# A hybrid attention and DeltaNet layer: one more pair of projections, one pass fewer, and two steps moved

## The chip, the cores and the metric

The kernel runs on one core of one Trainium2 chip. The metric is the time on the device in microseconds (us); TensorE does the matmuls, VectorE (DVE), ScalarE (ACT) and GpSimd (POOL) the elementwise work, SyncE (SP) issues most DMAs. Each engine has a queue of its own, filled in the order in which the program was written; semaphores hold an instruction until its inputs are there.

## What is computed

The reference, cut to what matters for this change:

```python
h = rms_norm(x, norm_g)                      # x: 768 tokens (512 + 256) of 2048 numbers
proj = einsum('bsd,dp->bsp', h, w_in)        # 8192 + 32 columns
aq, ak, av, ag, dq, dk, dv, dg, b_raw, a_raw = split(proj)
# attention: 8 heads x 128 from aq, ak, av, times silu(ag)
# DeltaNet:  8 heads x 128 from dq, dk, dv, times silu(dg); decay and beta per head and token:
beta = sigmoid(b_raw)
g = -exp(a_log) * softplus(a_raw + dt_bias)  # summed over a chunk, then exp: the decays
y = rms_norm(x + concat(attn, dn) @ w_out, final_gain)
```

All matmuls of the projection split both factors in two float32r parts (hi and lo) and add three products: hi by hi, hi by lo, lo by hi.

## The kernel before

x is kept transposed: 16 tiles of 128 rows (model dimension) by 768 tokens, each as `xh[k]` and `xl[k]`. `x_split` makes them from the landing buffer `xstage[k]` and multiplies by the norm gain `g_in` on the way (ScalarE for the high part, VectorE for the low one). The landing buffer itself keeps the plain x, for the sums of squares. The root of the mean square is applied to the results, by `rB`, a row of 768 factors that `start_rms` makes behind the first pass.

The 64 weight tiles of 128 columns are projected in four ways, in this order:

1. `project_two` with `ab=True`: two DeltaNet gates (tiles 56, 57) and the 32 columns for beta and decays (`ab_step`), tile of x by tile of x as they land. `arrivals` splits and squares each tile.
2. `project_two` again: gates 58, 59 (pass 2, `after="raw"`).
3. `project_two` again: q and k of attention head 0 (pass 3, `after="std"`).
4. `pair_products`: ten pairs of weight tiles, each in two halves (`ph`) of eight x tiles. A half uses seven products in place of eight, a Strassen-Winograd scheme over two blocks of tokens and two blocks of the model dimension. Its products (`PRODUCTS`) go into three PSUM banks X, Y, Z. `evacuate` takes each product out before the next one of the same bank starts. The products 4 to 7 multiply sums of x blocks, T1 to T4.
5. `project`: the convolution inputs of the DeltaNet and the other q and k, one tile at a time, beside which the attention and the scan run.

`block_sums(ph, i)` makes T1 to T4 for the x tiles a = 8 ph + i and a + 4, eight blocks in all. For one block it stores the second half of `xh[a]`, `xl[a]` to DRAM (`bD`), multiplies the two landing buffers by `g_in` (ScalarE), and then does four differences, four casts to the high part (ScalarE) and four low parts (VectorE). T2 takes the place of the second half of `xh[a]` and `xl[a]`, so it waits until the pass that counts in `reached["std"]` has used tile a:

```python
if n == "T2":
    yield from wait(lambda: reached["std"] > a)
    d[n] = xh[a][:, hi], xl[a][:, hi]
```

The others go to free landing buffers, listed in `PLACES`. At the last pair, `restore` loads the stored halves back.

The order of the instructions is planned while the program is built. `Driver` keeps a clock for each engine with the costs of `Engine.cost`. Side work is a set of generators, spawned with a priority (lower goes first): `follow` and `evacuate` -20, `arrivals` -10, `all_sums` -8, `spill_post`'s store -7, `gating` (beta and decays) -4. At each slot between matmuls, up to three steps of those that are due are written out. `yield AHEAD` lets a step go on 2 us before its own end by that plan, `yield 0` only at its end. Engines then run their queues in the order written.

`gating` waits for `rB`, multiplies the `ab` columns by it, transposes them on TensorE (`pg`), and does some 30 small operations on `scr` (96 columns) on VectorE with a few on ScalarE in between. Its last steps are small matmuls for the chunk sums and three exponentials. What it makes is used from the scan on, behind the pairs.

Of the kernel before, what the change touches and what calls it, by code (L numbers as in the profile page):

```python
# [16 lines left out]
T = 768  # L17
TP, TS = 512, 256
NT = T // P
NH = 8  # L20
# [32 lines left out]
AHEAD = 2.0  # L53
DEEP = 2.5
PAIRED = 0
# [202 lines left out]
def encoder_kernel(tc, x, xT, wt, wab, wo, convw, gain, dngain, fgain, alog, dtb, cst, tabs, y):  # L258
# [43 lines left out]
    with (  # L302
# [62 lines left out]
        if True:  # L365
# [67 lines left out]
            def arrivals():  # L433

                for k in range(NK):
# [3 lines left out]
                    for c in parts if k == 0 else (slice(0, T),):  # L439
                        x_split(k, c)  # L440
# [145 lines left out]
            reached = {"raw": 0, "std": 0, "left": 0}  # L586
# [159 lines left out]
            def block_sums(ph, i):  # L746
# [8 lines left out]
                for k in (a, a + 4):  # L755
                    A.mul(xstage[k], xstage[k], g_in[:, k:k + 1])
                yield AHEAD
# [17 lines left out]
                def low(n, E=V):  # L775
# [20 lines left out]
            PLACES = (("t16", "t17", "t18"), ("t19", "t20", "t21"), ("t22", "t23", "t0"), ("t4", "t1", "t5"), ("t2", "t6", "t3"),  # L796
                      ("t7", "t8", "t12"), ("t9", "t13", "t10"), ("t14", "t11", "t15"))
# [99 lines left out]
            def gating():  # L897
                ident, ones = C["ident"], C["ones"]
                yield from wait(lambda: "rms" in flags)
                yield from get("t23", "f768", "sa")  # L900
                scr = st("t23", (7, 2 * nd), "scr")
                ab = f768("ab")
                w1, w2, w3, w4, gg = (scr[:, j].rearrange("p (d t h) -> p d t h", d=2, t=NT) for j in (0, 1, 2, 3, 6))
                raw = scr[:, 4:6].rearrange("p b (d t h) -> p b d t h", d=2, t=NT)
# [60 lines left out]
                give("t23", "sa")  # L965
# [532 lines left out]

            pairs += [(h, NH + h) for h in range(NH - PAIRED, NH)]
            kinds += [(("q", h), ("k", h)) for h in range(NH - PAIRED, NH)]  # L1500
            attn = [(f, spill_post(kind, h)) for h in range(NH - PAIRED) for f, kind in ((h, "q"), (NH + h, "k"))]
            first, attn = attn[:2], attn[2:]
# [13 lines left out]
            plan_raw([f for f, _ in first])  # L1516
# [47 lines left out]
            drv.end = 0.0  # L1564
            spawn(arrivals(), -10)
            spawn(start_rms(), -30)
            project_two((raw_gate_post(0, "t19"), raw_gate_post(1, "t20")), raw_hook, ab=True)
            give("t16", "t17", "t18")
            spawn(all_sums(), -8)
            spawn(gating(), -4)  # L1570
            project_two((raw_gate_post(2, "t21"), raw_gate_post(3, "t22")), lambda k: None, "raw")
            project_two([p for _, p in first], lambda k: None, "std")

            def pair_hook(pi):
                def hook(ph, pr):
# [243 lines left out]
```

## Time and profile before

| | us |
|---|---|
| median of 3 runs | 1657.13 |
| lowest, highest | 1653.51, 1657.84 |
| the profiled execution | 1661.15 |
| its span (first to last instruction) | 1659.4 |
| mean granted TensorE clock in it | 0.985 of full speed |

The profile shows one execution on one core. "Busy" is the time in which an engine executes; an instruction's row gives its start from the span's start, its length, and in brackets the idle time ahead of it on its engine with what ended it. The ends of matmuls are modelled and overlap the next one's start, so their listed length is longer than the distance from one to the next.

### The profile page before, as it was taken

To read this page: it belongs to the slowest core of one execution; us is meant where nothing else is said; L and a number is where in the kernel's file an instruction comes from. 1 tells how busy PE (TensorE), PEld (TensorE's weight loads), DVE (VectorE), ACT (ScalarE), POOL (GpSimd) and SP (SyncE) were. 2 spreads that over 40 slices of the span, in tenths; PEclk is the share of its full clock that TensorE was granted. 3 is DMA by queue.
4 is the path that set the end of the run, shared out by engine and by line. 5 is a ranking of instruction groups with operands and counts; after the bars stand their busy time and mean duration, and the time that the engine had idled before them with its cause. 6 is when DMAs were issued, how large, how long until landed. Compare 5 with 4: busy or idle time off the path is not lost.

```text
span 1659.4 us, 30160 instructions
## 1 busy us (share of the span) xinstructions
PE 1597.8 (96%) x11675; PEld 1411.5 (85%) x11675; DVE 934.0 (56%) x2003; ACT 799.6 (48%) x1800; POOL 237.2 (14%) x233
## 2 busy tenths in 40 slices
PE   7998999999999999999999999999999889999995
PEld 6887999999888898988888888888878678887874
DVE  6558877778445554556555555665355555444332
ACT  6655333434354565556455656545355554433322
POOL 0000000000222221222213121312110011111220
PEclk9998999999999999999999999999999899999998
DMA  6232232323423323222223332232335455646557
GB/s 244 80 122 86 99 105 94 110 89 116 164 83 91 83 71 94 79 78 92 78 67 92 100 80 75 77 84 91 102 125 178 149 172 172 194 137 225 156 171 276
DMA packets 135265, 198.51 MB, mean 120 GB/s; under 512 B 49393, under 2 KB 60241, under 8 KB 135121
## 3 DMA queue, kind: packets, MB, share of 16 engines
q1 hardware_dynamic: 133968, 193.43, 36.2%
q10 hardware_dynamic: 1152, 3.15, 0.5%
q8 instruction: 92, 1.51, 0.4%
q14 instruction: 53, 0.43, 0.1%
HBM read 150.08 MB, written 46.45 MB: 118 GB/s over the span
## 4 chain that ended last, share of the span: by engine, by line
PE 80%; DMA 6%; DVE 5%; issue 4%; ACT 3%; POOL 1%; SPq 1%; ACTq 0%; DVEq 0%; POOLq 0%
PE mm L286 36%; PE mmo L286 8%; PE mmY L286 7%; PE mmr L286 7%; PE c L286 5%; PE mmX L286 5%; PE mmZ L286 5%; PE m L286 2%; DMA out_y<-row 2%; DMA st<-in_wo 1%; PE kk L286 1%; PE o L286 1%; DMA ak<-kD 1%; PE S L286 1%; DMA res<-in_x 1%
## 5 line engine op out<-in xcount | busy, mean ns | idle before, releaser
L286 PE MATMUL mm<-xl_x,hip 128*128 128x512 f32 (+1 forms) x1152 | 307.2, 348 | 0.0
L286 PE MATMUL mm<-xh_x,lop 128*128 128x512 f32 (+1 forms) x1152 | 305.5, 346 | 0.0
L286 PE MATMUL mm<-xh_x,hip 128*128 128x512 f32 (+1 forms) x1152 | 304.5, 345 | 0.0
L204 ACT CAST hip<-st 128x512 fp32r<-128x512 f32 x244 | 150.9, 619 | 236.8 <-PE mm L286 74.2
L204 POOL TENSOR_TENSOR lop<-st,hip 128x512 fp32r<-128x512 f32 x72 | 97.3, 1351 | 928.4 <-ACT hip L204 826.3
L204 DVE TENSOR_TENSOR lop<-st,hip 128x512 fp32r<-128x512 f32 x172 | 120.9, 703 | 193.8 <-ACT hip L204 188.6
L286 PEld LDWEIGHTS mm<-xh_x,hip 128*128 128x128 f32 x1152 | 176.5, 189 | 22.8
L286 PEld LDWEIGHTS mm<-xh_x,lop 128*128 128x128 f32 x1152 | 176.6, 189 | 21.7
L286 PEld LDWEIGHTS mm<-xl_x,hip 128*128 128x128 f32 x1152 | 176.4, 189 | 21.2
L286 PE MATMUL mmr<-xh_x,raw 128*128 128x512 f32 (+1 forms) x512 | 118.5, 345 | 11.3 <-ACT xh_x L204 9.6
L204 DVE SCALAR_TENSOR_TENSOR cacc<-cin,cw,cacc 128x772 f32<-128x772 f32 x96 | 107.4, 1119 | 23.4 <-ACT cacc L204 22.0
L204 ACT ACTIVATE s<-s,m 128x512 f32<-128x512 f32 (+1 forms) x96 | 61.5, 648 | 97.5 <-DVE m L204 97.4
L286 PEld LDWEIGHTS mmr<-xh_x,raw 128*128 128x128 f32 x512 | 79.7, 191 | 25.3 <-ACT xh_x L204 9.9
L286 PE MATMUL mmo<-oh,xh_m 128*128 128x512 f32 x192 | 79.2, 412 | 4.6 <-DVE q L204 4.1
L286 PE MATMUL mmo<-oh,mh 128*128 128x512 f32 x192 | 76.6, 399 | 1.8 <-ACT mh L204 1.6
L286 PE MATMUL mmo<-ol,xh_m 128*128 128x512 f32 x192 | 76.8, 400 | 1.0 <-POOL ol L204 0.5
L286 PE MATMUL mmo<-ol,mh 128*128 128x512 f32 x192 | 76.6, 399 | 0.6 <-DVE ol L204 0.5
L286 PE MATMUL mmo<-oh,ml 128*128 128x512 f32 x192 | 76.6, 399 | 0.3 <-DVE ml L204 0.3
L286 PE MATMUL mmo<-oh,xl_m 128*128 128x512 f32 x192 | 76.2, 397 | 0.0
L286 PE MATMUL mmr<-xl_x,raw 128*128 128x512 f32 (+1 forms) x256 | 67.0, 343 | 0.4 <-DVE xl_x L204 0.4
L204 ACT ACTIVATE z<-c,rho 128x128 f32<-128x128 f32 x96 | 35.1, 367 | 66.6 <-PE c L286 66.5
L204 DVE TENSOR_TENSOR res<-mmo,res 128x512 f32<-128x512 f32 x42 | 28.8, 687 | 67.5 <-PE mmo L286 46.3
(256 smaller groups left out, 3287.0 us busy)
## 6 DMA issues: line engine op xcount, KB each, us to landing
st<-in_wt SPq DMA_DIRECT2D x256, 256.0 KB
st<-in_wo SPq DMA_DIRECT2D x64, 256.0 KB
dec<-gcD SPq DMA_DIRECT2D x24, 256.0 KB
res<-in_x SPq DMA_DIRECT2D x24, 256.0 KB
yD<-res SPq DMA_DIRECT2D x24, 256.0 KB
res<-yD SPq DMA_DIRECT2D x24, 256.0 KB
out_y<-row SPq DMA_DIRECT2D x12, 512.0 KB
xst<-in_xT SPq DMA_DIRECT2D x15, 384.0 KB
```

Source lines behind the costliest of these rows:

```text
L204: r = f(*a, **k)
L286: r = PE.matmul(out, lhsT, rhs, start=start, stop=stop, skip_group_check=more)
```

## The change

- `PAIRED = 1`: q and k of head 0 become an eleventh pair, at the end of the pairs, in place of the third pass. `reached["std"]` is counted by the second pass now.
- `scales()`, a generator of its own at priority -7, multiplies the landing buffers by `g_in` as soon as their squares are taken. `block_sums` waits for two entries of `scaled` in place of doing it.
- `gating` waits for the flag `tset` (all block sums written out) in place of `rms`, and its scratch is in two `half` buffers in place of `t23`.
- The first part of x tile 0 is split ahead of the tasks; gates 2 and 3 go to `f768` buffers in place of `t21`, `t22`; `PLACES` is a new list.

```diff
-PAIRED = 0
+PAIRED = 1
@@ arrivals
-                    for c in parts if k == 0 else (slice(0, T),):
-                        x_split(k, c)
+                    x_split(k, slice(0, T) if k else parts[1])
@@ block_sums
-                for k in (a, a + 4):
-                    A.mul(xstage[k], xstage[k], g_in[:, k:k + 1])
-                yield AHEAD
+                yield from wait(lambda: {a, a + 4} <= scaled)
@@ new
+            scaled = set()
+
+            def scales():
+
+                for k in (0, 4, 1, 5, 2, 6, 3, 7, 8, 12, 9, 13, 10, 14, 11, 15):
+                    yield from wait(lambda: sq[0] > k)
+                    A.mul(xstage[k], xstage[k], g_in[:, k:k + 1])
+                    scaled.add(k)
+                    yield AHEAD
+
-            PLACES = (("t16", "t17", "t18"), ("t19", "t20", "t21"), ("t22", "t23", "t0"), ...
+            PLACES = (("t16", "t17", "t18"), ("t21", "t22", "t0"), ("t4", "t1", "t5"), ...
@@ gating
-                yield from wait(lambda: "rms" in flags)
-                yield from get("t23", "f768", "sa")
-                scr = st("t23", (7, 2 * nd), "scr")
+                yield from wait(lambda: "tset" in flags)
+                yield from get("half", "half", "f768", "sa")
+                scr, scr2 = (st("half", (4, 2 * nd), n) for n in ("scr", "scr2"))
@@ the lists of pairs and of single tiles
-            pairs += [(h, NH + h) for h in range(NH - PAIRED, NH)]
-            kinds += [(("q", h), ("k", h)) for h in range(NH - PAIRED, NH)]
-            attn = [(f, spill_post(kind, h)) for h in range(NH - PAIRED) for f, kind in ((h, "q"), (NH + h, "k"))]
-            first, attn = attn[:2], attn[2:]
+            pairs += [(h, NH + h) for h in range(PAIRED)]
+            kinds += [(("q", h), ("k", h)) for h in range(PAIRED)]
+            attn = [(f, spill_post(kind, h)) for h in range(PAIRED, NH) for f, kind in ((h, "q"), (NH + h, "k"))]
@@ the passes
+            x_split(0, parts[0])
             spawn(arrivals(), -10)
             spawn(start_rms(), -30)
+            spawn(scales(), -7)
             project_two((raw_gate_post(0, "t19"), raw_gate_post(1, "t20")), raw_hook, ab=True)
             give("t16", "t17", "t18")
             spawn(all_sums(), -8)
             spawn(gating(), -4)
-            project_two((raw_gate_post(2, "t21"), raw_gate_post(3, "t22")), lambda k: None, "raw")
-            project_two([p for _, p in first], lambda k: None, "std")
+            project_two((raw_gate_post(2, "f768"), raw_gate_post(3, "f768")), lambda k: None, "std")
```

## Rows read from the trace of the kernel before

**Rows 1.** The page, part 1: busy time, share of the span, instructions.

```profile
PE 1597.8 (96%) x11675; PEld 1411.5 (85%) x11675; DVE 934.0 (56%) x2003; ACT 799.6 (48%) x1800; POOL 237.2 (14%) x233
```

**Rows 2.** Windows by stage: from:to, length, busy time of each engine with its instructions, granted TensorE clock, share of the DMA engines, GB/s. Nearly all of pass 2; pass 3; pair 0 in two halves; pair 1.

```profile
63.49:97.20 33.71, 33.38 (x198) 29.12 (x198) 13.80 (x42) 13.35 (x34) 0.00 (x0) 1.00 0.25 80
96.30:130.19 33.89, 33.89 (x193) 29.23 (x192) 23.15 (x50) 22.09 (x43) 0.00 (x0) 1.00 0.38 125
130.19:155.11 24.92, 19.25 (x86) 18.51 (x85) 21.38 (x41) 13.32 (x25) 0.00 (x0) 0.80 0.33 113
155.11:171.88 16.77, 15.62 (x86) 14.76 (x85) 15.36 (x30) 8.07 (x15) 0.00 (x0) 0.99 0.22 76
171.88:200.98 29.10, 29.10 (x168) 28.86 (x168) 22.51 (x39) 9.84 (x17) 0.00 (x0) 1.00 0.29 101
```

**Rows 3.** Waits of TensorE from 0 to 200 us: who waited for whom, total us, times, longest.

```profile
PE mmr L286 <- ACT xh_x L204: 9.6, 1, 9.6
PE mmX L286 <- ACT sum L204: 3.5, 1, 3.5
PE mmY L286 <- DVE out L204: 2.7, 2, 2.2
...
PE mmY L286 <- DVE xl_x L204: 0.5, 1, 0.5
PE mmr L286 <- DVE xl_x L204: 0.4, 1, 0.4
```

**Rows 4.** TensorE's instructions in order of time, around pair 0: start, length, what, and in brackets the idle time ahead with its releaser.

```profile
132.11 0.34 PE L286 MATMUL mmX<-xh_x,lop 128*128 128x384 f32 x1
135.96 0.69 PE L286 MATMUL mmX<-xh_x,hip 128*128 128x384 f32 x1 [3.51 <-ACT sum L204]
...
137.09 0.52 PE L286 MATMUL mmX<-xh_x,hip 128*128 128x384 f32 x1
...
169.69 0.59 PE L286 MATMUL mmY<-T4s,hip 128*128 128x384 f32 x2 [0.58 <-DVE out L204]
```

**Rows 5.** VectorE's instructions in order of time, first and last ones of some blocks of the sums (T1f to T4f are the differences, T1s to T4s the low parts).

```profile
62.91 0.55 DVE L204 TENSOR_TENSOR T1f<-xst 128x384 f32<-128x384 f32 x1
...
103.36 0.55 DVE L204 TENSOR_TENSOR T4s<-T4f,T4s 128x384 fp32r<-128x384 f32 x1
...
105.72 0.55 DVE L204 TENSOR_TENSOR T1f<-xst 128x384 f32<-128x384 f32 x1
...
109.13 0.55 DVE L204 TENSOR_TENSOR T4s<-T4f,T4s 128x384 fp32r<-128x384 f32 x1
...
113.20 0.55 DVE L204 TENSOR_TENSOR T1f<-xst 128x384 f32<-128x384 f32 x1
...
160.73 0.55 DVE L204 TENSOR_TENSOR T4s<-T4f,T4s 128x384 fp32r<-128x384 f32 x1
```

**Rows 6.** VectorE's groups from 130.19 to 171.9 us: count, busy time, mean ns, idle time ahead. Of the eight kinds of operation of the block sums, T1f and T3f occur three times here and the other six four times; one of each count is shown.

```profile
L204 DVE TENSOR_TENSOR T1s<-T1f,T1s 128x384 fp32r<-128x384 f32 x4 | 2.2, 551 | 0.0
...
L204 DVE TENSOR_TENSOR T1f<-xst 128x384 f32<-128x384 f32 x3 | 1.7, 552 | 0.1
...
L204 DVE TENSOR_TENSOR k<-mmr,rB 128x512 f32<-128x512 f32 (+1 forms) x2 | 1.0, 549 | 0.0
```

**Rows 7.** ScalarE's instructions in order of time, at TensorE's stall of 3.51 us.

```profile
135.02 0.51 ACT L204 CAST T4s<-T4f 128x384 fp32r<-128x384 f32 x1 [2.22 <-DVE T4f L204]
135.43 0.47 ACT L204 COPY sum<-mmX 128x384 f32<-128x384 f32 x1
```

**Rows 8.** VectorE in the last pair: one evacuation and what it waited for.

```profile
419.86 0.56 DVE L204 TENSOR_TENSOR out<-mmY,sum 128x384 f32<-128x384 f32 x1 [2.01 <-DMA gD<-out]
```

**Rows 9.** The timeline in pass 3: ScalarE's scaling of two landing buffers, and three of VectorE's waits for a raw weight cast.

```profile
102.95 1.76 ACT L204 ACTIVATE xst<-xst,g_in 128x768 f32<-128x768 f32 x2
...
105.04 0.76 DVE L204 TENSOR_TENSOR raw<-st,raw 128x256 fp32r<-128x256 f32 x2 [1.14 <-ACT raw L204]
...
111.43 0.43 DVE L204 TENSOR_TENSOR raw<-st,raw 128x256 fp32r<-128x256 f32 x1 [1.08 <-ACT raw L204]
...
119.07 0.43 DVE L204 TENSOR_TENSOR raw<-st,raw 128x256 fp32r<-128x256 f32 x1 [1.24 <-ACT raw L204]
```

**Rows 10.** Waits of VectorE from 96.3 to 130.19 us: total, times, longest.

```profile
DVE raw L204 <- ACT raw L204: 5.9, 5, 1.5
DVE lop L204 <- PE mmr L286: 2.5, 1, 2.5
```

**Rows 11.** VectorE's groups from 63 to 100 us, those of the decays (`scr`): count, busy time, mean ns, idle time ahead and its releaser.

```profile
L204 DVE SCALAR_TENSOR_TENSOR scr<-scr 128x96 f32<-128x96 f32 x10 | 2.6, 258 | 0.3
...
L204 DVE TENSOR_SCALAR scr<-scr 128x96 f32<-128x96 f32 x4 | 0.8, 209 | 1.7 <-ACT scr L204 1.7
L204 DVE RECIPROCAL beta<-scr 128x96 f32<-128x96 f32 x1 | 0.8, 753 | 0.0
...
L204 DVE TENSOR_TENSOR scr<-scr,pg 128x96 f32<-128x96 f32 x2 | 0.5, 255 | 1.6 <-ACT scr L204 1.6
...
L204 DVE TENSOR_SCALAR ngc<-pg 128x96 f32<-128x96 f32 x1 | 0.3, 258 | 4.2 <-ACT scr L204 4.2
```

**Rows 12.** Waits of ScalarE in the first pass, from 9 to 52 us.

```profile
ACT raw L204 <- PE mmr L286: 7.4, 6, 2.4
ACT raw L204 <- DMA st<-in_wt: 4.0, 1, 4.0
```

More of the change, by code (lines that the diff above doesn't have):

```diff
@@ L583, in plan_pair @@
                             for pr in order)
-            reached = {"raw": 0, "std": 0, "left": 0}
+            reached = {"std": 0, "left": 0}
             def project_two(posts, before, after=None, ab=False):
@@ L794, in block_sums @@
                 yield AHEAD
-            PLACES = (("t16", "t17", "t18"), ("t19", "t20", "t21"), ("t22", "t23", "t0"), ("t4", "t1", "t5"), ("t2", "t6", "t3"),
-                      ("t7", "t8", "t12"), ("t9", "t13", "t10"), ("t14", "t11", "t15"))
+            scaled = set()
[5 more added lines that the diff above has]
+                    yield AHEAD
+            PLACES = (("t16", "t17", "t18"), ("t21", "t22", "t0"), ("t4", "t1", "t5"), ("t2", "t6", "t19"), ("t20", "t3", "t7"),
+                      ("t8", "t12", "t9"), ("t13", "t10", "t14"), ("t23", "t11", "t15"))
             def all_sums():
@@ L898, in gating @@
                 ident, ones = C["ident"], C["ones"]
-                yield from wait(lambda: "rms" in flags)
-                yield from get("t23", "f768", "sa")
-                scr = st("t23", (7, 2 * nd), "scr")
+                yield from wait(lambda: "tset" in flags)
+                yield from get("half", "half", "f768", "sa")
+                scr, scr2 = (st("half", (4, 2 * nd), n) for n in ("scr", "scr2"))
                 ab = f768("ab")
-                w1, w2, w3, w4, gg = (scr[:, j].rearrange("p (d t h) -> p d t h", d=2, t=NT) for j in (0, 1, 2, 3, 6))
-                raw = scr[:, 4:6].rearrange("p b (d t h) -> p b d t h", d=2, t=NT)
+                w1, w2, w3, w4 = (scr[:, j].rearrange("p (d t h) -> p d t h", d=2, t=NT) for j in range(4))
+                gg = scr2[:, 2].rearrange("p (d t h) -> p d t h", d=2, t=NT)
+                raw = scr2[:, 0:2].rearrange("p b (d t h) -> p b d t h", d=2, t=NT)
                 pg = side_ps("pg")
@@ L964, in gating @@
                 V.tensor_scalar(out=negegc, in0=egc, scalar1=-1.0, scalar2=None, op0=ALU.mult)
-                give("t23", "sa")
+                give("half", "half", "sa")
                 flags.add("gating")
@@ L1515, in encoder_kernel @@
             plan_raw((58, 59))
-            plan_raw([f for f, _ in first])
             for pi in range(len(pairs)):
```

## The prediction

> **What bounds the kernel now.** I read the page first: TensorE is busy for 96% of the span, VectorE for 56% [rows 1], so a gain must come from fewer matmul columns or from the few places where TensorE waits. The windows by stage come next. The third pass (q and k of head 0, 192 matmuls) takes 33.89 us with TensorE busy throughout. A pair in its steady state takes 29.10 us for the same two outputs, with 168 matmuls. The first pair, the two stretches from 130.19 to 171.88, takes 41.69 us: 12.6 us more than its successor, with the granted clock at 0.80 in its first half [rows 2]. TensorE's waits up to 200 us name what ended them: 3.5 us for ScalarE's copy of the first product, 2.7 us for VectorE's `out`, 0.5 us for a sum's low part [rows 3]: 6.7 of the 12.6 us. The rest is the clock. In TensorE's timeline a matmul of 384 columns is listed with 0.34 us before the stall of 3.51 us and with 0.52 us after it; behind the stall of 0.58 us at 169.69 two of them take 0.59, as at full clock [rows 4]. An idle microsecond of this stage cost 12.6/6.7 = 1.9 us in all, where the single stalls were long.
>
> Why it waits: the block sums T1 to T4 are late. VectorE makes block 0's first difference at 62.91 us, but T2 may overwrite x only when the pass that sets `reached["std"]` has used that x, and that is the third: block 0 ends at 103.9, block 7 at 161.3 us [rows 5]. So in the second pass VectorE is busy for 13.80 of 33.71 us [rows 2], and at the start of pair 0 30 of the 64 VectorE operations of the sums are still to come (three or four of each of the eight kinds, and the spill of k [rows 6]). They are in one queue with the weight sums and the evacuations. ScalarE's copy of product 1, whose matmuls end at 132.45 [rows 4], starts at 135.43, behind the T4 cast, which waits 2.22 us for VectorE's T4f [rows 7].
>
> **The change, part by part.**
>
> *Third pass out, eleventh pair in.* Minus 33.89, plus a steady pair of 29.10 [rows 2]: -4.8 us. The weight loads are eight of 256 KB either way. VectorE gets a pair's 22.5 us, inside a steady stretch where TensorE never waits. The last pair of before has a stall of its own, where `out` waits 2.01 us for a store [rows 8] that stands behind the restoring loads of SP's queue. The new last pair issues the same loads behind the same kind of store, so I leave it: 0, between -4 (gone, at 1.9 each) and +4 (doubled).
>
> *Sums beside the second pass.* `std` is now set by pass 2, so the sums meet the same grid as before: the release of x some 4 us into a pass of 33.9 us, first need just behind it. What differs is the scaling. In the third pass ScalarE's scaling (1.76 us for two tiles) stood ahead of the raw weight casts, and VectorE, whose queue is in order, waited for those casts: 1.14, 1.08 and 1.24 us at 105.04, 111.43 and 119.07 [rows 9], 3.5 of its 5.9 us of such waits [rows 10]. A block's eight operations take 4.0 us from 105.72 on when nothing stops them [rows 5], 0.49 each, so the freed time holds seven more. I expect 23 operations, 11.3 us, left at the start of pair 0 instead of 30 (14.7). With them come about 1.5 us for the last raw gates' products in place of 1.0 us of k: 12.8 against 15.7 us. Before, 15.7 us of extra work became 6.7 us of idle, so 9.0 were absorbed; 12.8 would leave 3.8, at 1.9 each 7.2 us. Below, if all 5.9 us and the wait of 2.5 us for a weight buffer [rows 10] are used, 13 operations and 1.5 us, 7.9 in all, are left, less than is absorbed: 0. Above, if the pace stays, 14.7 and 1.9: 7.6 x 1.9 = 14.4 us. I take 7.2: the waits behind the scaling are rows, the others may stay.
>
> *Decays behind the sums.* They leave pass 2, where nobody needed VectorE, and enter pairs 0 and 1. TensorE's part of them (the small matmuls and transposes of `pg`) only changes place. VectorE's operations add up to about 8.3 us (ten of 0.26 us, two reciprocals of 0.75 us, two products on `ab` of 0.5 us, a dozen others of 0.2), and between them it stood for ScalarE 1.6, 1.7 and 4.2 us in pass 2 [rows 11]. Part of that would pass beside older work in a full queue; with 5 us of waits the step blocks VectorE for 13.3 us. Behind a waiting decay operation stand the evacuations that release the banks X, Y, Z, and TensorE waits for those. The cover is VectorE's idle time in a steady pair, 29.10 - 22.51 = 6.6 us [rows 2]. Spread over 1.3 pairs (38 us, an estimate: the step goes on only as its own last operation ends), 8.6 us are covered and 4.7 us come through, in stalls short enough to keep the clock. Below, over two pairs, 13.2 are covered: 0. Above, over one pair and with the clock lost, 6.7 x 1.9 = 12.7 us. I take 4.7, since the longest batch, some 15 operations, is shorter than the two products (4.2 us) between most evacuations and the next use of their bank, but not than the one product between the seventh and the fourth.
>
> *Pair 0's excess*, with what spills into pair 1, thus goes from 12.6 to 7.2 + 4.7 = 11.9 us: -0.7.
>
> *Scaling as x lands.* Sixteen operations of 0.88 us [rows 9], 14 us, enter ScalarE's first pass. It waited there for 7.4 + 4.0 us in 43 [rows 12], so some 2.6 us don't fit. Behind a scaling stand the next x splits; TensorE waited for one of those only 0.4 us after its start [rows 3]. I take 0, at most +2.6. *First half of x split ahead of the weights:* ScalarE does it before the casts that wait for their DMA, up to 0.5 us off TensorE's first wait of 9.6 us [rows 3], but at 32 us TensorE waits for tile 7, behind a cast that the DMA held for 4.0 us [rows 12], and would wait that much longer: 0. *Raw gates in f768* in place of `t21`, `t22`: the buffers that q and k held before, for about as long: 0.
>
> *Sum:* -4.8 - 0.7 = -5.5 us. The profiled execution took 1661.15 us (span 1659.4), 4.0 above the median of 1657.13; from its own time the sum gives 1655.7, and at the median 1651.6 us. About 0.3%, 5 us, is what a measurement of this kernel can tell from no change.
>
> **The rivals.**
>
> 1. *The sums are done in time and the decays are covered.* VectorE has 20 idle us in the second pass, and the decays' 8 beside them; if it uses most, seven or eight of the eight blocks are done by pair 0. The excess is then about 1.5 (the copy between products 1 and 2, which stand next to each other in the first order) + 1: 2.5 instead of 12.6, so -14.9: 1642. For it: eight blocks of 4.0 us fit in 33.9. Against it: blocks 1 and 2 began 7.5 us apart, at 105.72 and 113.20 [rows 5], and only part of that was scaling.
>
> 2. *The pace of the sums stays.* The casts' waits move elsewhere in the queue, the excess of the sums remains 12.6, the decays add 4.7, and the pass saves 4.8: 1657, no change. For it: the longest wait of VectorE in the third pass, 2.5 us for a weight buffer that TensorE still read [rows 10], has nothing to do with the scaling.
>
> 3. *Slower: the decays hold up the evacuations.* Each decay batch waits inside for ScalarE or TensorE, and the next bank's evacuation is late by the whole batch. Unabsorbed, that is 13.3 us; pair 0 lost 5.9 us to the clock over two long stalls, so one more such stall makes it 16.3, in place of 4.7: -5.5 + 11.6 = +6.1, 1663. It decides from the point where the decays cost more than 4.7 + 5.5 = 10.2 us; below that the change is not slower. For it: the copy that ScalarE could have run at 132.45 started at 135.43 us behind a cast [rows 7]. Against it: the idle time of two steady pairs equals the whole step. The Trainium skill speaks for this rival ("TensorE: Matmul & The Clock Gate", Architectural detail, on queue depths: only TensorE pulls a weight load ahead of running work, ScalarE and VectorE are strict FIFO). The trace agrees, by that same copy behind its cast; by the rule alone, with no idle time to give way, the change would end at this rival's 1663 us.
>
> **How the numbers follow.** Forecast (1648 to 1656) 0.42; rival 1 0.18; rival 2 0.26; rival 3 0.14. The range 1642 to 1662 leaves out most of rival 3 and the lower half of rival 1, about 0.2; it takes in an excess from 2.5 to some 22 us, not both upper bounds (14.4 + 12.7) at once. Faster by over 0.3% means under 1652.2: 0.7 of the forecast and rival 1, and a tenth of rival 2 (0.49); within 0.3%: 0.3 of the forecast, most of rival 2 (0.37); slower: rival 3 (0.14).
>
> **What would show it.** In the trace after: steady pairs of 29.1 us, ten in all; blocks of the sums about 6 us apart, block 7's T4 some 12 to 17 us into pair 0; no `xst` scaling beside the sums; TensorE's waits for `sum`, `out` or `pg` in pairs 0 and 1 of 6 to 8 us together; `scr` operations between evacuations. The prediction would be wrong by a pair 0 of under 33 us (rival 1), by sums that end over 25 us into it (rival 2), or by stalls of over 2 us each that end on an `out` behind `scr` (rival 3). A first pass in which TensorE waits for `xh_x` after 33 us would be the scaling's fault.

## The result, and the profile after

The changed kernel takes 1675.96 us (median of four runs, 1673.56 to 1675.99) against 1657.47 us for the kernel before on the same chip: a ratio of 1.0111, with an interval of 1.0099 to 1.0124. The forecast was 1651.6 with a range of 1642 to 1662: the sign is wrong, and the time lies above the range. The profiled execution took 1675.93 us, with a span of 1674.2.

Windows of the kernel after, by stage (columns as in [rows 2]): the first 59 us, the second pass, pair 0 in its two halves, a steady pair.

```profile
0.00:59.00 59.00, 46.81 (x233) 37.53 (x234) 35.30 (x52) 44.94 (x69) 0.34 (x6) 0.94 0.51 181
67.57:101.00 33.43, 33.43 (x192) 29.44 (x193) 22.64 (x49) 17.35 (x39) 0.00 (x0) 1.00 0.36 126
101.00:128.67 27.67, 15.70 (x74) 14.50 (x73) 22.01 (x42) 12.16 (x24) 0.00 (x0) 0.84 0.31 110
128.67:156.15 27.48, 23.01 (x103) 22.01 (x104) 22.07 (x46) 9.43 (x20) 0.00 (x0) 0.81 0.18 59
188.00:217.10 29.10, 29.10 (x168) 28.86 (x168) 22.67 (x38) 9.73 (x17) 0.00 (x0) 1.00 0.29 100
```

The reader is to see three things. The second pass begins at 67.57 us; before it began at 59.0. The second pass itself takes 33.43 us with TensorE never waiting. And pair 0 takes 55 us where [rows 2] have 41.7: TensorE is busy for 15.70 of 27.67 and 23.01 of 27.48 us, at a granted clock of 0.84 and 0.81, while VectorE is busy for 80% of both halves.

Waits of TensorE from 0 to 200 us in the kernel after, the answer to [rows 3]:

```profile
PE mmY L286 <- DVE out L204: 9.4, 2, 6.2
PE mmr L286 <- ACT raw L204: 7.2, 1, 7.2
PE mmr L286 <- ACT xh_x L204: 5.5, 3, 3.0
PE mmX L286 <- ACT sum L204: 4.5, 1, 4.5
...
PE pg L291 <- DVE ab L204: 0.9, 1, 0.9
```

Added up by stage, in the two profiled executions (us): start of the second pass +8.6; second pass 37.3 to 33.4, -3.9 (the decays' matmuls left it); third pass -33.9; one more pair +29.3; pair 0 41.7 to 54.9, +13.2; pair 1 29.3 to 32.2, +2.9; last pair 33.0 to 29.9, -3.1. The sum is +13.1, and the pairs end at 452.37 instead of 439.02. The medians differ by 18.5 rather than by this: the profiled execution of before was itself 3.7 us above its median of 1657.47, and 1.4 us more come behind the pairs.

Two of these places are named by rows. In the first pass ScalarE's scalings of two landing buffers stand right ahead of a split of x, for which TensorE then waits (3.00 us up to 35.09, 1.11 us up to 60.49). ScalarE of the kernel after, in order of time, and TensorE's second wait:

```profile
32.46 1.76 ACT L204 ACTIVATE xst<-xst,g_in 128x768 f32<-128x768 f32 x2
34.12 0.92 ACT L204 ACTIVATE xh_x<-xst,g_in 128x768 fp32r<-128x768 f32 x1
...
57.85 1.76 ACT L204 ACTIVATE xst<-xst,g_in 128x768 f32<-128x768 f32 x2
59.52 0.92 ACT L204 ACTIVATE xh_x<-xst,g_in 128x768 fp32r<-128x768 f32 x1
```

```profile
60.49 0.61 PE L286 MATMUL mmr<-xh_x,raw 128*128 128x512 f32 x2 [1.11 <-ACT xh_x L204]
```

The same wait of 1.11 us, near 60 us, stands in all four kernels below that scale on ScalarE in the first pass, and in no other. The one at 35.09 is not the scaling's alone: ten of the eleven kernels that don't scale in the first pass wait for `xh_x` for 0.3 to 3.3 us between 32 and 34 us. In scale_in_block, where the split stands right behind a weight cast that waited for its DMA, the row is

```profile
32.65 0.98 PE L286 MATMUL mmr<-xh_x,raw 128*128 128x512 f32 x2 [2.61 <-ACT xh_x L204]
```

Windows of the first pass, the kernel after and then the kernel before. From 30 to 40 us TensorE does half of the matmuls, at a granted clock of 0.71 against 1.00; from 50 to 60 us ScalarE is busy for 9.94 us, where before it had 2.9 us to spare.

```profile
30.00:40.00 10.00, 6.96 (x27) 5.14 (x26) 5.63 (x9) 8.56 (x13) 0.00 (x0) 0.71 0.30 103
50.00:60.00 10.00, 9.38 (x55) 7.53 (x53) 5.96 (x9) 9.94 (x15) 0.00 (x0) 1.00 0.16 49
```

```profile
30.00:40.00 10.00, 9.56 (x54) 7.61 (x53) 8.82 (x13) 8.42 (x15) 0.00 (x0) 1.00 0.30 101
50.00:60.00 10.00, 10.00 (x55) 7.94 (x54) 3.04 (x7) 7.13 (x12) 0.00 (x0) 1.00 0.09 26
```

The second place is beside the sums. ScalarE's cast of T2 into x waits for the store that saves that half of x first; six such waits add up to 11.7 us, where the kernel before had one of 1.5. Three of them:

```profile
81.80 0.51 ACT L204 CAST xh_x<-T2f 128x384 fp32r<-128x384 f32 x1 [2.43 <-DMA bD<-xh_x]
89.18 0.51 ACT L204 CAST xh_x<-T2f 128x384 fp32r<-128x384 f32 x1 [2.20 <-DMA bD<-xh_x]
...
123.76 0.51 ACT L204 CAST xh_x<-T2f 128x384 fp32r<-128x384 f32 x1 [2.78 <-DMA bD<-xh_x]
```

The store of the last one left SP's queue at 119.92 us, right behind a weight load. In the kernel before, the 1.76 us of scaling stood in ScalarE's queue ahead of the block's differences and casts; in its blocks 1 to 7 the cast of T2 began some 4 us or more behind the issue of the store, and waited for it once.

VectorE's groups from 101 to 157 us in the kernel after: T4s occurs five times, the other seven kinds of the sums four times each (T1f shown), so 33 operations of the sums were left when pair 0 began, and two products of the raw gates (the operations counted in the same way as the 30 of [rows 6]):

```profile
L204 DVE TENSOR_TENSOR T4s<-T4f,T4s 128x384 fp32r<-128x384 f32 x5 | 2.8, 552 | 0.0
...
L204 DVE TENSOR_TENSOR T1f<-xst 128x384 f32<-128x384 f32 x4 | 2.2, 551 | 0.0
...
L204 DVE TENSOR_TENSOR gated<-gated,rB 128x768 f32<-128x768 f32 x2 | 1.9, 952 | 0.0
```

### The profile page after: what moved, and what is told of

Read it like the earlier page. It is cut to its first block, busy times and chain, and to the rows that moved or that the text cites. A ratio compares the mean times of both kernels' runs of the same rounds, so it can differ in the third digit from the quotient of the medians.

```text
span 1674.2 us, 30144 instructions
## 1 busy us (share of the span) xinstructions
PE 1597.9 (95%) x11651; PEld 1413.8 (84%) x11651; DVE 947.6 (57%) x2021; ACT 803.9 (48%) x1801; POOL 238.6 (14%) x233
## 4 chain that ended last, share of the span: by engine, by line
PE 77%; DMA 8%; DVE 5%; ACT 4%; issue 3%; SPq 1%; POOL 1%; ACTq 0%; DVEq 0%; POOLq 0%
PE mm L286 35%; PE mmo L286 8%; PE mmY L286 8%; PE mmX L286 5%; PE mmZ L286 5%; PE c L286 5%; PE mmr L286 3%; PE m L286 2%; DMA out_y<-row 2%; DMA st<-in_wo 1%; PE kk L286 1%; PE o L286 1%; DMA xst<-in_xT 1%; PE S L286 1%; DMA ak<-kD 1%
## 5 line engine op out<-in xcount | busy, mean ns | idle before, releaser
L204 ACT CAST hip<-st 128x512 fp32r<-128x512 f32 x254 | 157.0, 619 | 250.6 <-PE mm L286 83.7
L204 DVE TENSOR_TENSOR lop<-st,hip 128x512 fp32r<-128x512 f32 x182 | 127.5, 701 | 205.3 <-ACT hip L204 203.4
L286 PE MATMUL mmr<-xh_x,raw 128*128 128x512 f32 (+1 forms) x384 | 91.3, 348 | 15.5 <-ACT raw L204 7.3
L286 PEld LDWEIGHTS mmr<-xh_x,raw 128*128 128x128 f32 x384 | 61.0, 194 | 27.3 <-ACT raw L204 7.8
L204 ACT ACTIVATE z<-c,rho 128x128 f32<-128x128 f32 x96 | 35.1, 367 | 66.9 <-PE c L286 66.7
L286 PE MATMUL mmX<-xh_x,hip 128*128 128x384 f32 x176 | 60.4, 343 | 4.5 <-ACT sum L204 4.5
```

What stands on the lines that cost most here:

```text
L204: r = f(*a, **k)
L286: r = PE.matmul(out, lhsT, rhs, start=start, stop=stop, skip_group_check=more)
```

## The experiments

All of them change the kernel after, but for the last three, which change the kernel before. The table gives the ratio to the kernel before of the same chip with its interval, and from the profiled execution where the second pass begins, its length, the lengths of pairs 0 and 1 and where the pairs end (us).

| kernel | median | ratio | pass 2 from | pass 2 | pair 0 | pair 1 | pairs end |
|---|---|---|---|---|---|---|---|
| before | 1657.5 | | 59.0 | 37.3, then 33.9 | 41.7 | 29.3 | 439.0 |
| after | 1676.0 | 1.0111 (1.0099 to 1.0124) | 67.6 | 33.4 | 54.9 | 32.2 | 452.4 |
| scale_in_block | 1675.4 | 1.0113 (1.0094 to 1.0131) | 60.8 | 34.1 | 54.0 | 39.5 | 452.5 |
| decay_early | 1668.5 | 1.0067 (1.0051 to 1.0084) | 69.0 | 36.8 | 48.9 | 29.3 | 448.0 |
| store_ahead | 1671.5 | 1.0084 (1.0063 to 1.0104) | 67.6 | 34.1 | 45.4 | 37.3 | 448.7 |
| scale_pool | 1678.8 | 1.0134 (1.0114 to 1.0153) | 73.3 | 33.3 | 55.1 | 32.6 | 459.2 |
| pair_only | 1664.7 | 1.0046 (1.0031 to 1.0061) | 61.8 | 37.1 | 53.4 | 29.3 | 445.8 |
| three_mended | 1665.8 | 1.0053 (1.0036 to 1.0069) | 59.4 | 37.1 | 51.3 | 29.3 | 441.4 |
| decay_late | 1668.9 | 1.0071 (1.0056 to 1.0086) | 62.9 | 33.4 | 50.9 | 29.3 | 446.3 |
| low_act | 1664.9 | 1.0044 (1.0029 to 1.0059) | 66.9 | 33.4 | 45.9 | 32.7 | 443.6 |
| pair_pad | 1661.4 | 1.0021 (1.0005 to 1.0036) | 61.3 | 37.0 + 14.6 | 36.2 | 29.3 | 442.7 |
| pair_order | 1667.7 | 1.0061 (1.0043 to 1.0078) | 59.8 | 38.0 | 52.7 | 29.3 | 444.1 |
| pair_double | 1681.4 | 1.0137 (1.0117 to 1.0157) | 61.7 | 37.1 | 67.4 | 29.3 | 459.8 |
| before_early | 1656.6 | 0.9996 (0.9981 to 1.0011) | 62.1 | 71.5 with pass 3 | 40.0 | 29.3 | 438.6 |
| before_early_v | 1655.7 | 0.9985 (0.9970 to 0.9999) | 61.8 | 70.6 with pass 3 | 37.9 | 29.3 | 435.2 |
| early_later | 1654.3 | 0.9972 (0.9959 to 0.9984) | 59.1 | 70.6 with pass 3 | 37.9 | 29.3 | 431.9 |

One profiled execution can lie several us off its kernel's median (three_mended's took 1660.3 against 1665.8, early_later's 1650.4 against 1654.3), so the last column does not rank the kernels. The kernels that don't scale in the first pass begin the second anywhere from 59.0 to 62.9 us.

**scale_in_block.** The scalings go back into the blocks of the sums.

```diff
-                yield from wait(lambda: {a, a + 4} <= scaled)
+                for k in (a, a + 4):
+                    A.mul(xstage[k], xstage[k], g_in[:, k:k + 1])
+                yield AHEAD
...
-            spawn(scales(), -7)
```

> The changed kernel with the scaling back inside the blocks of the sums (two tiles on ScalarE at the start of each block); everything else stays changed. Theory A, from the two traces: the scaling as x lands is what makes the first pass 8.6 us longer (pass 2 starts at 67.57 instead of 59.01 us), since one or two scalings stand right ahead of an x split in ScalarE's queue. Then pass 2 starts at 59 to 60 us again. Theory B: inside a block the scaling used to pass the time in which the store of x to bD is under way; without it ScalarE's cast of T2 waits for that store (six waits, 11.7 us). Then these waits shrink to under 3 us in all here, and the distance of two blocks stays near 7.5 us, scaling in place of waiting. Both together: about 1667 us, some 8 to 9 less than the changed kernel's 1676. Rival C (VectorE simply has more work than time around pair 0, whatever ScalarE does): the first pass may shrink, but what it gives is lost again in pair 0, so 1674 to 1677.

The second pass begins 6.8 us earlier, and the waits for stores shrink to one of 1.3 us: both A and B hold in their places. But the time is the same, 1675.4 us. What was gained comes back in pairs 0 and 1, 54.0 and 39.5 us. The sums end in pair 0, and most of the decays, which follow them, stand in pair 1; it has one stall of 3.29 us and a granted clock of 0.87. Windows of scale_in_block, pairs 0 and 1:

```profile
94.86:148.90 54.04, 39.27 (x177) 36.46 (x176) 42.13 (x79) 27.72 (x50) 0.00 (x0) 0.84 0.24 84
148.90:188.40 39.50, 35.88 (x186) 35.27 (x185) 27.85 (x60) 10.73 (x24) 0.00 (x0) 0.87 0.22 75
```

VectorE is busy for 70 of these 93.5 us. The time is inside C's 1674 to 1677: a gain ahead of pair 0 that is given back behind it is theory C's mark.

**decay_early.** The decays go back into the second pass, with their work area in `t23` as before.

```diff
-                yield from wait(lambda: "tset" in flags)
-                yield from get("half", "half", "f768", "sa")
...
+                yield from wait(lambda: "rms" in flags)
+                yield from get("t23", "f768", "sa")
...
```

> The changed kernel with the decays back in pass 2 (they wait for rB again and use t23); everything else stays changed. If the decays behind the sums cost what the traces suggest (waits of 3.2 + 0.9 + 0.3 us for out, ab and pgt in the second half of pair 0, and the clock of 0.81 there), 1668 to 1670 us. Rival C (VectorE has too much work in pass 2 and pair 0 together): the decays then push the sums back by their 8 us and the waits between, pair 0 waits for T2 or T1 of its second half, and the time stays at 1676 or rises.

7.5 us faster. Pair 1 is a steady pair again and pair 0 is 6.0 us shorter: 8.9 us together, of which the second pass takes 3.4 back for the decays' own matmuls. 1668.5 is what the traces' waits had suggested, and not C's 1676 or more.

**store_ahead.** Each block's store of x is issued one block earlier.

```diff
...
+                        if 4 * ph + i < 7:
+                            store(4 * ph + i + 1)
                         yield from block_sums(ph, i)
```

> The changed kernel with the store of a block's half of x to bD issued one block earlier than the block needs it; nothing else differs. Theory B (the cast of T2 waits for that store, and ScalarE's queue makes the weight casts and VectorE wait with it): the six waits of 11.7 us vanish, blocks come 5 to 6 us apart instead of 7.5 to 8, block 7 ends 10 us earlier or more, pair 0's excess falls from 25.9 to 10 to 15 us, and the kernel takes 1662 to 1666. Rival C (VectorE's work is the bound): ScalarE's waits vanish, but the blocks stay where they are and the gain is under 3 us: 1673 to 1676.

4.5 us faster, between B's 1662 to 1666 and C's 1673 to 1676. The waits for stores are gone but for one of 1.2 us, block 7 ends 8 us earlier, and pair 0 is 9.5 us shorter; then the decays, which follow block 7, make pair 1 5.1 us longer. B is a cost, and about half of what it frees is lost again.

**scale_pool.** The scalings stay in the first pass, on GpSimd.

```diff
-                    A.mul(xstage[k], xstage[k], g_in[:, k:k + 1])
+                    G.tensor_tensor(out=xstage[k], in0=xstage[k], in1=g_in[:, k:k + 1].to_broadcast([P, T]), op=ALU.mult)
```

> The changed kernel with the sixteen scalings of the landing buffers on GpSimd, which has nothing to do in the first pass, at the same places of the plan. Theory A (ScalarE's queue is what the scalings cost): pass 2 starts at 59 to 60 us, and 1667 us in all. Rival: if GpSimd and VectorE get in each other's way at their access to the memory, VectorE's low parts of x (1.02 us each) get longer in the first pass and the gain is smaller; if pass 1 is long for another reason (the loads, the split of the first half), it stays at 67 us.

Slower still: the second pass begins at 73.3 us. TensorE has a new wait of 6.2 us for VectorE's `xacc`, since VectorE's operations take longer while GpSimd multiplies (last section). The experiment did not isolate A: it replaced ScalarE's cost by another one.

**pair_only.** Scalings in the blocks and decays in the second pass, the edits of scale_in_block and decay_early together: the pairing is what is left.

> The pairing alone: the scalings are back inside the blocks of the sums (that block of two scalings ahead of each block's casts) and the decays back in the second pass. Theory A+B (the scalings in the first pass cost 6 to 8 us there; inside the blocks they cover the store of x): pass 1 ends near 60 us, ScalarE's casts of T2 wait for stores once or not at all, and with the 7.5 us that the decays gave back the time is 1676 - 8 - 7.5 = about 1660. Theory C (VectorE has the sums' 35 us to do behind the first pass, and what the first pass gains is given back in pair 0): the gain of the first pass is lost again, 1668, as with the decays alone back. The prediction's own step for the pairing (-4.8 us, sums no later than before) would give 1652 to 1653.

1664.7 us lies between the answers of A (1660) and C (1668). The first pass is mended, no cast waits for a store, no decay stands in a pair; and pair 0 still takes 53.4 us. So the pairing, with the new places of the sums and the split of x that came with it, costs 7.7 us (against the kernel before of the same chip, 1657.06), where the forecast had -4.8 for it. And against scale_in_block, which differs in the decays alone, it is 10.7 us faster: the decays cost more here than the 7.5 us of decay_early.

**three_mended.** As pair_only, with the edit of store_ahead.

> All three suspected costs taken out of the changed kernel: scalings inside the blocks, stores of x one block ahead, decays in the second pass. If the single effects add (-6 in the first pass, -9 in pair 0 from the stores, -7.5 from the decays): about 1654. Theory C: what the first pass and the stores give, VectorE's queue keeps for the larger part, since its work behind the first pass is the same: 1663 to 1666, with pair 0 still over 40 us.

1665.8 us, inside what C said, and no better than pair_only: with the scaling as cover the early store gives nothing. Its longest stall, of 8.1 us, shows how the sums reach TensorE. ScalarE of three_mended:

```profile
102.26 0.84 ACT L204 ACTIVATE gated<-gated 128x768 f32<-128x768 f32 x1
...
103.41 0.51 ACT L204 CAST T4s<-T4f 128x384 fp32r<-128x384 f32 x1
105.53 0.84 ACT L204 ACTIVATE gated<-gated 128x768 f32<-128x768 f32 x1 [1.61 <-DVE gated L204]
106.28 0.46 ACT L204 COPY sum<-mmX 128x384 f32<-128x384 f32 x1
```

The copy that TensorE wants stands behind a Silu that waits for VectorE's product on a gate, and VectorE does that product behind the sums.

**decay_late.** As three_mended, with the decays held until the fourth pair.

> As the kernel with all three taken out, but the decays start only with the fourth pair, where the sums are long done. If a steady pair covers them (6.6 us of idle time of VectorE in 29.1, the prediction's cover): pairs 0 and 1 as without decays, the fourth pair at most 2 us longer, and the second pass 3 to 4 us shorter for want of the decays' matmuls: 3 to 6 us under the kernel with all three taken out. If the decays hold up evacuations wherever they stand (rival 3): the fourth pair takes 34 to 37 us and the time is no better than with the decays in the second pass.

The cover fails: pair 3 takes 35.4 us instead of 29.3. Waits of TensorE in it:

```profile
PE mmX L286 <- DVE lop L204: 1.1, 1, 1.1
PE pgt L291 <- ACT scr L204: 1.0, 1, 1.0
PE mmZ L286 <- DVE sum L204: 0.7, 1, 0.7
```

These are 2.7 of the 6.1 us; the other 3.4 are the decays' own matmuls, as in the second pass. So where nothing else is late the decays cost 2.7 us in stalls. The fourth pair and the time are what the expectation gave for rival 3.

**low_act.** On store_ahead; the low parts of T1, T3 and T4 are left out, and 24 copies by ScalarE stand in their place.

```diff
-                    E.tensor_tensor(out=d[n][1], in0=t[n], in1=d[n][0].bitcast(F32), op=ALU.subtract)
...
+                    else:
+                        A.copy(d[n][1], t[n])
...
```

> The kernel with the stores one block ahead (1671.5 us), in which the low parts of T1, T3 and T4 are left out: ScalarE writes a copy of the difference in their place, so 24 operations of 0.55 us, 13.2 us, leave VectorE's queue beside pass 2 and pair 0 and 24 of some 0.5 us enter ScalarE's. Theory C (VectorE is what the sums wait for): most of it comes out of the 16 us that pair 0 and the 8 us that pair 1 are over: 1658 to 1661. If VectorE's amount of work is not what holds them (the order in the queues, ScalarE's casts, the release of x by pass 2): within 3 us of 1671.

6.6 us faster than store_ahead: neither C's 10 to 13 nor the rival's 3. The gain is in pair 1 (37.3 to 32.7), not in pair 0. Since the operations went into ScalarE's queue, on which VectorE waits in turn, this run doesn't separate amount from hand-over.

**pair_pad.** On pair_only: 84 matmuls nobody reads, between the second pass and pair 0.

```diff
...
+            for r in range(7):
+                for i in range(12):
+                    mm(pad[:, :HALF], xl[4 + i % 4][:, :P], xh[4 + i % 4][:, :HALF], start=(r == 0 and i == 0), stop=(r == 7 - 1 and i == 11),
+                       more=True)
+                    drv.slot()
...
```

> The pairing alone (1664.7 us, pair 0 of 53.4 us, 24.1 over a steady one), with 84 matmuls of 384 columns more between the second pass and pair 0, whose result nobody reads: 14.6 us of TensorE's time that ask nothing of VectorE and ScalarE. Theory C (pair 0 is long because the third pass was VectorE's room for the sums, and the room is gone): the sums go on beside them, pair 0 is shorter by nearly as much, 39 to 42 us, and the time stays within 3 us of 1664.7. Rival (pair 0's stalls come from its own order and queues, not from the amount of work that is left): pair 0 keeps its 53 us and the time is 1679.

1661.4 us: 14.6 us of added work cost nothing. The median is 3.3 us under pair_only's, though the intervals of the two ratios overlap, and pair 0 falls from 53.4 to 36.2 us, below C's 39 to 42; its granted clock goes from 0.84 to 0.95. Windows of pair_only (second pass, pair 0), and then of pair_pad (second pass, added matmuls, pair 0):

```profile
61.83:98.89 37.06, 36.73 (x217) 31.84 (x216) 28.95 (x73) 26.06 (x56) 0.00 (x0) 1.00 0.34 116
98.89:152.30 53.41, 36.63 (x171) 34.24 (x170) 40.77 (x75) 28.06 (x48) 0.00 (x0) 0.84 0.24 84
```

```profile
61.29:98.30 37.01, 36.68 (x217) 31.81 (x216) 28.87 (x73) 26.06 (x56) 0.00 (x0) 1.00 0.38 126
98.30:112.92 14.62, 14.62 (x87) 14.62 (x85) 11.18 (x21) 11.30 (x19) 0.00 (x0) 1.00 0.21 81
112.92:149.10 36.18, 31.50 (x169) 30.44 (x169) 29.61 (x55) 16.88 (x30) 0.00 (x0) 0.95 0.26 81
```

VectorE's work is the same in both, 28.95 + 40.77 = 69.7 and 28.87 + 11.18 + 29.61 = 69.7 us. In pair_only TensorE's own work in that stretch is 37.1 + 29.1 = 66.2 us, less than VectorE's, and VectorE needs 90.5 us with its waits. With the added matmuls TensorE's own work is 80.7, and the stretch is over after 87.8.

**pair_order.** On pair_only: the steady order of products in the first half of pair 0 too.

```diff
...
-                    pair_products(pi, ph, ORDER if pi or ph else FIRST_ORDER, kinds[pi], pair_hook(pi))
+                    pair_products(pi, ph, ORDER, kinds[pi], pair_hook(pi))
```

> The pairing alone, with the steady order of the products (1, 6, 5, 2, ...) in the first half of pair 0 too, so that products 1 and 2, which share a bank, don't stand next to each other: the stall of 7.9 us for ScalarE's copy goes. Theory D (that stall and the clock it costs are half of pair 0's excess): pair 0 of 42 to 45 us, 1655. Theory C (the sums end when VectorE has done them, whatever the order): product 6 waits for T2 of block 3 for some 3 us, the second half for block 7, and the time stays within 3 us of 1664.7.

D falls. The stall for the copy shrinks from 7.9 to 2.7 us, the waits for T2 (`xh_x`) grow from 3.5 to 9.3, and pair 0 takes 52.7 us. At 1667.7 us the time is that of pair_only within 3.

**pair_double.** On pair_only: VectorE writes each low part twice.

```diff
-                E.tensor_tensor(out=d[n][1], in0=t[n], in1=d[n][0].bitcast(F32), op=ALU.subtract)
+                [E.tensor_tensor(out=d[n][1], in0=t[n], in1=d[n][0].bitcast(F32), op=ALU.subtract) for _ in (0, 1)]
```

> The pairing alone (1664.7 us), with each of the 32 low parts of the sums written twice by VectorE: 17.6 us more for VectorE behind the first pass, no new hand-over between the engines. There VectorE is busy for 69.7 of the 90.5 us of the second pass and pair 0, TensorE's own work is 66.2. Theory C in its narrow form (VectorE's amount of work sets the end of pair 0): 12 to 17 us longer, 1677 to 1682. Rival (the hand-overs between VectorE and ScalarE, both queues in order, set it, and VectorE's 20.7 idle us take the rest): at most 4 us longer, 1665 to 1669.

1681.4 us, 16.6 more than pair_only by the medians (15.1 by the ratios) for 17.6 us of VectorE's work: the narrow form of C. Window of pair 0 of pair_double, and VectorE's two largest waits from its second pass to the end of pair 0:

```profile
98.84:166.24 67.40, 38.02 (x171) 34.50 (x170) 58.24 (x110) 31.97 (x56) 0.00 (x0) 0.75 0.21 75
```

```profile
DVE lop L204 <- ACT hip L204: 8.0, 7, 3.5
DVE raw L204 <- ACT raw L204: 7.2, 2, 6.8
```

VectorE is busy for 58.24 of 67.40 us. Its idle time in that stretch falls from 20.7 us in pair_only to 18.0 only, so it takes little of the added work; 15.2 of the 18.0 us VectorE stands for ScalarE's casts of weights (`hip`, `raw`), in a chain of two queues.

**before_early.** The kernel before: T2's difference is parked in the landing buffer, so that only its cast and low part wait for the third pass; the last raw gates go to `f768`, and `PLACES` is a new list.

```diff
-                yield from diff("T2", xb[:, hi], t["T1"])
-                yield from high("T2")
+                V.tensor_tensor(out=xa[:, hi], in0=xb[:, hi], in1=t["T1"], op=ALU.subtract)
+                spawn(last_of(), -9)
...
```

> The kernel before, third pass and all, but the sums use VectorE's idle time in the second pass: a block waits for the third pass's release of x with its T2 alone (the difference is parked in the landing buffer and cast later), and the last two raw gates go to f768, so that their landing places are free for sums. Theory C: some 14 operations of the sums, 7 us, move from behind the start of pair 0 into the second pass (13.8 us of VectorE busy in 33.7 there), pair 0's excess falls from 12.6 to 1 to 4 us: 1646 to 1650. If the amount of sums left at the start of pair 0 isn't what stretches it: 1657.

1656.6 us, no measurable change, where C had 1646 to 1650: C missed, and the time is the one expected if the amount of sums left is not what stretches pair 0. Four blocks begin in the second pass, and 12 operations are left at the start of pair 0 in place of 30; but the other four blocks still come 10 us apart in the third pass and pair 0, and pair 0 is 1.7 us shorter only.

**before_early_v.** The same, with a pair of v tiles last.

```diff
+            pairs.append(pairs.pop(3))
+            kinds.append(kinds.pop(3))
```

> As the kernel before with the early sums, and the pair of the last two v tiles is moved from the fourth place to the last, where two gates stood, whose outputs go through a Silu before they are stored. In the kernel before the last pair takes 33.0 us, in every kernel whose last pair is q and k of head 0 29.6 to 30.4. If the kind of the last pair is what does it: 3 us under the kernel with early sums alone. If it isn't (the restoring loads of x stand ahead of a store in any case): the same time.

The kind of the last pair is not what does it: it takes 30.6 us with gates last and 30.4 with v last, 33.0 only in the kernel before. 1655.7 us, at the edge of what can be told.

**early_later.** The same, with the parked T2 cast put into the queues two x tiles later.

```diff
-                    yield from wait(lambda: reached["std"] > a)
+                    yield from wait(lambda: reached["std"] > min(a + 2, NK - 1))
```

> The kernel before with early sums and v last (1655.7 us), with the parked T2 cast put into the queues two x tiles later than the third pass's release, so that ScalarE and VectorE don't stand behind a cast that TensorE has not released (2.8 us each at 118 us there). If the sums that are left at the start of pair 0 (two blocks there) stretch it by 8.6 us: nearly all blocks end in the third pass, pair 0 takes 30 to 33 us, 1648 to 1651. If the rest of the excess is pair 0's own (products 1 and 2 next to each other): 36 to 38 us and 1654 to 1656.

1654.3 us, 0.28% under the kernel before, with an interval that lies below 1: faster than both kernels, by about the least that can be told, and in the profiled execution mostly through the last pair and pair 0, 3.0 and 3.8 us shorter than before. Pair 0 stays at 37.9 us. That is what the expectation gave if the rest of the excess is pair 0's own. But blocks still follow each other at some 10 us and 12 operations of the sums are left at its start, where the expectation had nearly none, so the question put to it, whether pair 0 loses all its excess without sums, stays open.

## Why the prediction was wrong

*Third pass out, eleventh pair in: right.* -33.9 + 29.3 is -4.6 against -4.8; eight pairs of 29.3 us stand there behind pairs 0 and 1. The last pair's term, left at 0 between -4 and +4, came out at -3.1. Why the last pair of the kernel before alone stalls was not settled.

*Sums beside the second pass: the step that failed.* Its term was an excess of 7.2 us in pair 0; decay_early's pair 0, which has no decays, takes 19.8 us over a steady 29.1. The step reckoned 23 operations left at the start of pair 0; there were 33 in the kernel after (groups from 101 us) and 36 in decay_early. The sums of the kernel after end 37 us into pair 0, past the 25 us that the text set as rival 2's mark:

```profile
137.75 0.55 DVE L204 TENSOR_TENSOR T4s<-T4f,T4s 128x384 fp32r<-128x384 f32 x1
```

The step took ScalarE's scaling as a cost to VectorE that would go [rows 9]. It also was the cover of x's store, whose latency stands in no term: without it the casts of T2 wait 11.7 us, and the blocks began 7 to 11 us apart, where the list expected 6. scale_in_block and store_ahead both show these waits go. With 36 operations and 1.9 us of gate products the step's own formula gives (36 x 0.49 + 1.9 - 9.0) x 1.9 = 20.0 us, beside decay_early's 19.8. So there the price per operation held and the count was wrong.

The price does not hold at smaller counts. pair_pad has 20 operations left, and an excess of 7.1 us where the formula gives 1.5; early_later has 12, and 8.8 us where it gives none. So the reading of pair 0 of the kernel before, that the sums left over make its 12.6 us, holds for a part: 18 operations fewer took 3.8 us off. TensorE of early_later still waits for the copy of the first product; why is open.

```profile
135.25 0.69 PE L286 MATMUL mmX<-xh_x,hip 128*128 128x384 f32 x1 [3.26 <-ACT sum L204]
```

Curing the store did not save the change. The deeper fault is the frame: the step compared stalls and pace and never set VectorE's whole work against TensorE's. From the second pass to the end of pair 0 the kernel after has 22.64 + 22.01 + 22.07 = 66.7 us of VectorE's work to 33.4 + 29.1 = 62.5 of TensorE's. The kernel before had 77.6, from 59.01 to 171.88 us, to about 100 of TensorE's (37.1 + 33.9 + 29.1):

```profile
59.01:171.88 112.87, 105.72 (x578) 94.52 (x576) 77.62 (x167) 60.39 (x120) 0.00 (x0) 0.95 0.31 103
```

The third pass was VectorE's room. pair_pad (room given back: 14.6 us of work at no cost) and pair_double (work added: most of 17.6 us comes through) show it, for the chain that VectorE and ScalarE form: the stretch takes 88.4 us in the kernel after, some 22 more than VectorE's work. Whether the amount of VectorE's work or the hand-overs set the pace of that chain was not separated: low_act leaves it open, and before_early speaks against the amount alone. This is rival 2 with a worse end than its 1657: the pace of the sums stayed, and 20 idle us of the second pass [rows 2] were not enough, since raw low parts, gate products and four blocks filled it to 22.64 of 33.43.

*Decays: mis-sized, and close to rival 3.* 4.7 us were taken, with 10.2 as the point where the change turns slower. They cost 8.9 us in pairs 0 and 1, and 7.5 at the median; with the scalings in the blocks (scale_in_block against pair_only) they cost 10.7, past that point. (The list of VectorE's operations in that step adds up to 7.5 us, not to its 8.3; the trace of before has 8.2.) Rival 3's mark is there, one stall of over 2 us on an `out` behind `scr`. VectorE of the kernel after, and TensorE's row that waited for it:

```profile
150.18 0.75 DVE L204 RECIPROCAL scr<-scr 128x96 f32<-128x96 f32 x1
150.97 0.55 DVE L204 TENSOR_TENSOR scr<-scr 128x96 f32<-128x96 f32 x2
151.44 0.69 DVE L204 TENSOR_TENSOR lop<-st,hip 128x512 fp32r<-128x512 f32 x1
152.04 0.55 DVE L204 TENSOR_TENSOR out<-mmY,sum 128x384 f32<-128x384 f32 x1
```

```profile
152.74 0.59 PE L286 MATMUL mmY<-T4s,hip 128*128 128x384 f32 x2 [3.21 <-DVE out L204]
```

The longer stall, 6.22 us up to 128.67, ends on an `out` behind the late T2 cast, not behind a decay. In scale_in_block a `sum` comes late behind a batch of twelve operations on `scr` (from 155.73 us). TensorE's two rows, of the kernel after and of scale_in_block:

```profile
128.67 0.98 PE L286 MATMUL mmY<-T4s,hip 128*128 128x384 f32 x2 [6.22 <-DVE out L204]
```

```profile
162.73 0.66 PE L286 MATMUL mmZ<-xh_x,hip 128*128 128x384 f32 x1 [3.29 <-DVE sum L204]
```

That TensorE's part of the decays only changes place held (-3.9 in the second pass, 3.4 in decay_late's fourth pair). The cover, 6.6 idle us of VectorE in a steady pair, was too good: 2.7 us come through even there.

*Scaling as x lands: wrong by its upper bound.* 0 was taken, at most 2.6; the start of the second pass moved by 8.6 us in the two profiled executions. The four kernels that scale on ScalarE in the first pass begin the second at 66.9 to 69.0 us, the eleven others without it, the kernel before among them, at 59.0 to 62.9; the means are 6.9 us apart. ScalarE's 14 us were set against its idle time of 11.4 us [rows 12], as if order did not matter; but two scalings in a row hold up the next split of x by 1.76 us, and from 50 to 60 us ScalarE was busy for all but 0.06 us. The text's own mark, a wait for `xh_x` after 33 us, is in the trace at 35.09 and 60.49; the first doesn't tell, since kernels without these scalings have it too (before_early waits 1.44 us up to 33.43), the second does.

Yet the single costs don't come back one by one. scale_in_block begins the second pass 6.8 us earlier, rids the casts of nearly all waits for stores, and gains 0.6 us; store_ahead's pair 0 is 9.5 us shorter, and it gains 4.5. With the decays back in the second pass the scaling in the first costs 3.7 us (decay_early against pair_only, with ratios whose intervals overlap); with the decays behind the sums it costs nothing that can be told. In that order the 18.5 us of the change are 7.7 for the pairing and 10.7 for the decays. What these runs show is that time given back ahead of pair 0 is for the most part spent in pairs 0 and 1.

## What to carry to other kernels

Before a stage is taken out because another does its work with fewer matmuls, add up for each engine the work that must be done between the first point where it can start and the first point where it is needed; if the removed stage was the room of a second engine, its TensorE time is not there to be saved. Work that looks like an obstacle in a queue may be what covers a DMA's latency, so look for what was issued just ahead of it. Where single repairs don't add up, test for room directly: add work that leaves the suspected engine alone, and double that engine's work.

## What was not expected of the hardware

GpSimd's multiply of two SBUF tiles slows VectorE's operations. VectorE's groups from 9 to 66 us, first of the kernel after, then of scale_pool:

```profile
L204 DVE SCALAR_TENSOR_TENSOR xl_x<-xst,g_in,xh_x 128x768 fp32r<-128x768 f32 (+1 forms) x16 | 15.7, 982 | 11.3 <-ACT xh_x L204 11.3
```

```profile
L204 DVE SCALAR_TENSOR_TENSOR xl_x<-xst,g_in,xh_x 128x768 fp32r<-128x768 f32 (+1 forms) x16 | 23.3, 1458 | 1.1 <-ACT xh_x L204 1.1
```

Single ones, VectorE and GpSimd of scale_pool in order of time:

```profile
23.62 2.22 DVE L204 SCALAR_TENSOR_TENSOR xl_x<-xst,g_in,xh_x 128x768 fp32r<-128x768 f32 x1
...
42.15 1.01 DVE L204 SCALAR_TENSOR_TENSOR xl_x<-xst,g_in,xh_x 128x768 fp32r<-128x768 f32 x1
```

```profile
22.79 12.41 POOL L204 TENSOR_TENSOR xst<-xst,g_in 128x768 f32<-128x768 f32 x6 [9.98 <-ACT sq L204]
```

Beside GpSimd's run of multiplies the operation takes 2.22 us, without one 1.01. The Trainium skill ("SBUF — State Buffer", Who interferes with whom) says that a VectorE instruction with two SBUF inputs contends with a GpSimd instruction that reads SBUF, and that the ports which the two share are an exclusive lock. That there is contention, this trace shows; whether one waits for the other's whole instruction it doesn't, since no idle time is shown ahead of the longer operations: what they lose is in their busy time.
